# Attention stage: scores in four quarters of the PE array, merge weights sent a step earlier, a shorter end

## Chip, cores and metric

The kernel runs on one core of a Trainium2 chip. The metric is the time of one execution in microseconds of device time; a run's figure is the median of its executions. Lower is better.

## What is computed

A two-layer trunk on 1024 tokens of width 1024. Layer 0 is a gated short convolution, layer 1 dilated sliding-window attention in three groups (window and dilation 128/1, 512/4, 2048/16), 16 heads of 64 in each. The change lies in layer 1.

```python
def dilated_group_attention(q, k, v, bias_tab, window, dilation):
    # the sequence is split into `dilation` residue classes, each cut into 128-query blocks
    logits = einsum('brhnqd,brhnkd->brhnqk', qs, kb) * HEAD_DIM ** -0.5   # kb: past block and own block
    step = BLOCK + a - kk                                                 # a: query row, kk: 0..255
    valid = (step >= 0) & (step <= span) & (key_pos >= 0)                 # span = window // dilation = 128
    logits = where(valid, logits + bias, -inf)
    lse = logsumexp(logits, axis=-1)
    out = einsum('brhnqk,brhnkd->brhnqd', exp(logits - lse[..., None]), vb)
    return out, lse

def dilated_attention_mixer(h, w_in, q_gain, k_gain, w_out, rel_bias):
    ...
    alpha = softmax(stack(lses, axis=0), axis=0)          # merge weights of the three groups
    o = sum(alpha[..., None] * stack(outs, axis=0), axis=0)
    return (o * silu(z)) @ w_out
```

A query row `a` of a block sees keys `a` to `a + 128` of the 256 in past and own block.

## The kernel before

All data lie with features on the partitions. The convolution layer and the projections of the attention layer run first (three-product fp32r matmuls of fast matrix schemes); they write queries, keys (`qkd`), values (`vd`) and gates (`zd`) to DRAM. Then the attention stage follows, whose order is written by hand: the code emits instructions in the order in which each engine shall run them.

Work is cut into 24 units: head pair `hp` (0 to 7, two heads in partitions 0 to 63 and 64 to 127) by group `g` (0 to 2). Units of groups 0 and 1 have four steps of two blocks, group 2 has two steps of four blocks: ten steps a head pair, 80 in all, numbered k. In group 0 all blocks but the first have a past block, in group 1 four of eight, in group 2 none (`alone`). Each step has three parts at fixed distances (lags):

- A (lag 0): scores, one matmul for each block and head: 64 rows of the head (the two heads in the two row halves of PE), 128 queries as weights, 128 or 256 keys as moving columns, into banks `ps` (pool `sp`, three banks, two used by a step). DVE adds the bias and takes the row maxima (L899, `xs`, `nl`), ACT exponentiates and sums (L902). The bias is -1e30 on keys outside the window.
- B (lag `LB` = 2): PE transposes (L909, `pt`, two banks), ACT and DVE copy to `pts` (L847, L849).
- C (lag `LC` = 4): values times `pts` into `po` (L928, and L922 for group 2, 128 rows by 64 columns, the heads in the two column halves); the last step of a half copies `po` to `O` (L939, `finish`).

The rest of a head pair is hung on the last step of its group 2 (`end`) with lags: `store` (maxima and sums to DRAM `nld`, and for group 2 back as `ml` in another layout, L945 on POOL's queue), `weights` (L959 to L963, DVE and ACT), `shares` (L972 to L977), `store_shares` (`fo` to DRAM `fd`), `spread(w)` (two broadcast DMAs of 256 KB from `fd` to `fb`, L985, pool `fbp` of two buffers), `scale(w)` (O times `fb`, DVE, L988), `add(w)` (POOL, L991), `gate` (times SiLU of z, DVE, L994), `high` and `low` (split for the three products, ACT L998 and DVE L1001). The last head pair spreads with PE instead (`wide`, `spread_last`, `last`).

The output projection is done in four parts of two head pairs (`some`, `dense`: six matmuls L1069 to L1071 a tile of 128 x 512, 16 tiles), one tile a step from `LD` steps after the first step of the next even head pair on; DVE adds each tile to `acc` (L1105, `add_sums` at the start of the next step). So steps 0 to 33, 50 to 53 and 70 to 73 have no dense products. Within a step the lags run in the order 0, 1, 4, 3, 5 to 14, 2, then the dense tile, then loads. After the last step the loop goes on until all lags and tiles are out, two tiles a step, with free score, transpose and output banks as further accumulators; then the last two head pairs (kt 6 and 7) are multiplied and closed, tile by tile.

Of the kernel before, what the change touches and what calls it, by code (L numbers as in the profile page):

```python
# [10 lines left out]
F32 = mybir.dt.float32  # L11
# [24 lines left out]
def trunk(ctx: ExitStack, tc: tile.TileContext, a, out):  # L36
# [775 lines left out]
    wp = ctx.enter_context(tc.tile_pool(name="wp", bufs=4, reuse_waits="tile"))  # L812
    with tc.tile_pool(name="sp", bufs=3, space=PSUM) as sp, tc.tile_pool(name="ptp", bufs=2, space=PSUM) as ptp, \
            tc.tile_pool(name="opp", bufs=2, space=PSUM) as opp, tc.tile_pool(name="pp1", bufs=1, space=PSUM) as pp1, \
# [21 lines left out]
        def load_v(hp, g):  # L836
            VS[hp, g] = ap.tile([P, 8, P], F32, name="V", tag="V", bufs=3)
            for q in range(2):
                nc.sync.dma_start(VS[hp, g][:, 4 * q:4 * q + 4].rearrange("p a b -> p (a b)"), vd[hp, g, q])

        O = {}
# [9 lines left out]
        def attention(hp, g):  # L851
# [21 lines left out]
            def make(js, first):  # L873
# [3 lines left out]
                def A():  # L877
                    if first:
                        begin()
                    q, k = QK[hp, g]  # L880
                    ps = [sp.tile([P, 4, P], F32, name="ps", tag="ps") for _ in range(2)]
                    todo = []
                    for n, j in enumerate(js):
                        alone = g == 2 or (j == 0 if g == 0 else j < 4)
                        x0, nk = (n if g == 2 else 2 * n), 1 if alone else 2
                        b = 2 * (j % 4) + j // 4 if g == 1 else j
                        vb = [b] if alone else [b - 1, b]
                        kv = slice(vb[0] * P, (b + 1) * P)
                        for s, hs in enumerate((lo, up)):
                            out_ = ps[s][:, x0:x0 + nk].rearrange("p a b -> p (a b)")  # L890
                            nc.tensor.matmul(out_, q[hs, b * P:(b + 1) * P], k[hs, kv], start=True, stop=True)  # L891
                        todo.append((x0, nk, j, slice(0 if nk == 2 or g == 2 else 128, 256 if nk == 2 or g < 2 else 128)))
                        c.extend((x0 + i, j, vb[i], i == 0, i == nk - 1) for i in range(nk))
# [88 lines left out]
            def spread(w):  # L982
                fb = u["fb", w] = fbp.tile([P, S], F32, name="fb", tag="fb")
                for s, hs in enumerate((lo, up)):
                    nc.gpsimd.dma_start(fb[hs], fd[hp, w, s][None, :].to_broadcast([64, S]))  # L985
# [28 lines left out]
            def spread_last(hf):  # L1014

                hs = slice(64 * hf, 64 * hf + 64)
                for w in (2, 1, 0):
                    fb = u["fb", w] = sp.tile([P, 4, P], F32, name="ps", tag="ps").rearrange("p a b -> p (a b)")
                    for r in range(8):
# [68 lines left out]
        def bank(name):  # L1088
            if name in ("pd", "po"):
                return (pp1 if name == "pd" else opp).tile([P, HALF], F32, name=name, tag=name)  # L1090
            pool = sp if name == "ps" else ptp
            return pool.tile([P, 4, P], F32, name=name, tag=name).rearrange("p a b -> p (a b)")

# [28 lines left out]
        for i, (dt, hf) in enumerate(tiles):  # L1122
            when(4 + i, residual, dt, hf)
        for r in range(3):
            k0 = at[2 * r + 2, 0][0] + LD
            k = k0
            for i, (dt, hf) in enumerate(tiles):
                late = k >= len(steps)
                name = "pd" if not late else ("pd", ("ps", "ps", "pt", "pt")[min(k - len(steps), 3)])[i % 2]
                extra.setdefault(k, []).append(lambda r=r, dt=dt, hf=hf, name=name:  # L1130
                                               some((2 * r, 2 * r + 1), dt, hf, name))
                k += i % 2 if late else 1
        for kt in range(KT):
            k = at[kt // 2 * 2 + 2, 0][0] + LD - 4 + kt % 2 if kt < 6 else len(steps) - 5 + kt % 2
            when(k - 4 - kt % 2, fetch, kt)
            when(k, split, kt)
            when(k + 1, split_low, kt)
        for f in begins.pop(-1):
            f()
        k = 0  # L1140
        while k < len(steps) + LC or any(x >= k for x in extra):
            add_sums()
# [102 lines left out]
```

## Time and profile before

| | us |
|---|---|
| median of 3 runs | 1992.55 |
| lowest and highest run | 1991.82, 1994.5 |
| the profiled execution | 1993.42 |
| its span | 1991.5 |
| PE busy | 1942.4 (98%) |
| DVE busy | 1484.1 (75%) |
| ACT busy | 903.5 (45%) |
| POOL busy | 885.3 (44%) |

The profile is of one execution. Busy shares are means over very different stages; the attention stage starts at 1625.89 us. A matmul of f32 stands as two records, a transpose as one. An engine's idle time is put down to what ended last before its next instruction; a record's own duration is longer than the distance to the next, since matmuls are pipelined, so costs on PE are read from start to start.

### The profile page before, as it was taken

What the parts mean: (1) busy time and instruction counts of PE and PEld (TensorE: products, weight loads), DVE (VectorE), ACT (ScalarE), POOL (GpSimd) and SP (SyncE); (2) the same over time, 40 slices, a digit from 0 to 9 for tenths busy, and PEclk for the clock granted to TensorE, in tenths of its full rate; (3) what the DMA queues carried; (4) which work ended last, traced back from release to release, by engine and by line L of the source; (5) the groups of instructions that cost most, each with busy time, mean ns of one, the idle gap of its engine ahead of it and who ended that gap; (6) DMA issues with size and microseconds to landing.
All of it is one profiled execution on the core that took longest, in us unless ns stands there. A gap on an engine that the chain in (4) does not pass through costs nothing.

```text
span 1991.5 us, 29494 instructions
## 1 busy us (share of the span) xinstructions
PE 1942.4 (98%) x10302; PEld 1579.2 (79%) x10302; DVE 1484.1 (75%) x2751; ACT 903.5 (45%) x2042; POOL 885.3 (44%) x800
## 2 busy tenths in 40 slices
PE   8999999999999999999999999999999998899998
PEld 6888888888887888788887888788888876677776
DVE  6866665666666555898888788878899856787886
ACT  6433333333335344534343434343443448777770
POOL 0356767667665112444455444544454442222330
PEclk9999999999999999999999999999999999999999
DMA  6313232232225565323333323332433278767752
GB/s 198 113 62 96 71 106 85 85 106 70 89 77 176 165 235 171 118 85 106 106 106 117 96 96 117 107 105 85 127 99 106 93 239 259 206 174 219 207 142 85
DMA packets 116805, 254.25 MB, mean 128 GB/s; under 512 B 15822, under 2 KB 22718, under 8 KB 116656
## 3 DMA queue, kind: packets, MB, share of 16 engines
q1 hardware_dynamic: 93024, 177.42, 28.4%
q0 software_dynamic: 23632, 74.95, 12.5%
q8 instruction: 81, 1.33, 0.3%
q14 instruction: 68, 0.56, 0.1%
HBM read 193.05 MB, written 67.64 MB: 131 GB/s over the span
## 4 chain that ended last, share of the span: by engine, by line
PE 77%; DVE 10%; issue 5%; DMA 4%; ACT 2%; POOL 1%; SPq 0%; DVEq 0%; POOLq 0%; ACTq 0%
PE pp L301 18%; PE pp L304 18%; PE pp L303 18%; PE pp L552 3%; PE pp L553 3%; PE pp L551 3%; DVE ws L165 2%; PE pt L909 2%; PE ps L891 2%; DMA nld<-nl 1%; DVE blkc L711 1%; PE pp L374 1%; PE pp L376 1%; PE pp L375 1%; PE po L928 1%
## 5 line engine op out<-in xcount | busy, mean ns | idle before, releaser
L165 DVE TENSOR_TENSOR ws<-wr,ws 128x512 fp32r<-128x512 f32 x284 | 265.3, 936 | 115.5 <-ACT ws L164 114.6
L164 ACT ACTIVATE ws<-wr 128x512 fp32r<-128x512 f32 x284 | 178.3, 629 | 360.4 <-PE pp L304 236.7
L276 POOL TENSOR_TENSOR sr<-wr 128x512 f32<-128x512 f32 x136 | 192.6, 1416 | 264.6 <-DMA wr<-in_conv_w_in 69.7
L164 ACT ACTIVATE ws<-sr 128x512 fp32r<-128x512 f32 x272 | 169.7, 629 | 285.5 <-PE pp L304 236.2
L165 DVE TENSOR_TENSOR ws<-sr,ws 128x512 fp32r<-128x512 f32 x272 | 227.6, 845 | 80.4 <-ACT ws L164 77.6
L313 DVE TENSOR_TENSOR f<-pp,f 128x512 f32<-128x512 f32 x204 | 139.5, 684 | 90.2 <-PE pp L304 83.3
L902 ACT ACTIVATE xs<-xs,nl 128x128 f32<-128x128 f32 (+1 forms) x384 | 167.9, 439 | 68.9 <-DVE nl L899 57.7
L309 ACT ACTIVATE f<-pp 128x512 f32<-128x512 f32 x228 | 132.7, 582 | 28.4 <-POOL blkc L683 14.5
L899 DVE CUSTOM_DVE_ANT_0 xs<-ps,bt 128x128 f32<-128x128 f32 (+1 forms) x384 | 110.9, 347 | 27.5 <-PE ps L891 16.3
L716 POOL DMA_DIRECT2D qkd<-blkc x96 | 68.1, 717 | 131.6 <-DVE blkc L711 123.0
L674 ACT ACTIVATE f<-f 128x512 f32<-128x512 f32 x96 | 60.7, 633 | 140.2 <-DVE f L313 103.1
L276 POOL TENSOR_TENSOR sr<-wr,sr 128x512 f32<-128x512 f32 x68 | 88.9, 1307 | 65.7 <-issue 43.4
L301 PE MATMUL pp<-blkg,ws 128*128 128x512 f32 x272 | 107.3, 394 | 4.3 <-ACT f L309 4.2
L301 PE MATMUL pp<-blkf,ws 128*128 128x512 f32 x272 | 108.5, 399 | 0.7 <-ACT f L309 0.7
L301 PE MATMUL pp<-blka,ws 128*128 128x512 f32 x272 | 107.1, 394 | 0.7 <-ACT f L309 0.7
L301 PE MATMUL pp<-blkb,ws 128*128 128x512 f32 x272 | 107.4, 395 | 0.0
L301 PE MATMUL pp<-blkd,ws 128*128 128x512 f32 x272 | 107.0, 393 | 0.0
L304 PE MATMUL pp<-blkf,ws 128*128 128x512 f32 x272 | 106.3, 391 | 0.0
L304 PE MATMUL pp<-blkd,ws 128*128 128x512 f32 x272 | 106.0, 390 | 0.0
L304 PE MATMUL pp<-blka,ws 128*128 128x512 f32 x272 | 106.0, 390 | 0.0
L304 PE MATMUL pp<-blkb,ws 128*128 128x512 f32 x272 | 106.0, 390 | 0.0
L301 PE MATMUL pp<-blke,ws 128*128 128x512 f32 x272 | 106.0, 390 | 0.0
(329 smaller groups left out, 5388.0 us busy)
## 6 DMA issues: line engine op xcount, KB each, us to landing
wr<-in_conv_w_in SPq DMA_DIRECT2D x128, 256.0 KB, 3.0
wr<-in_wqk SPq DMA_DIRECT2D x96, 256.0 KB, 3.1
qkd<-blkc POOLq DMA_DIRECT2D x96, 256.0 KB, 3.1
qk<-qkd SPq DMA_DIRECT2D x48, 512.0 KB, 8.6
wr<-in_conv_w_out SPq DMA_DIRECT2D x64, 256.0 KB, 3.1
f<-in_x SPq DMA_DIRECT2D x48, 256.0 KB, 4.3
wr<-in_wv SPq DMA_DIRECT2D x48, 256.0 KB, 3.0
vd<-f POOLq DMA_DIRECT2D x48, 256.0 KB, 2.5
```

What stands on the lines that cost most here:

```text
L164: nc.scalar.activation(t[:, 0], src, AF.Copy)
L165: nc.vector.tensor_tensor(t[:, 1], src, t[:, 0].bitcast(F32), op=OP.subtract)
L276: nc.gpsimd.tensor_tensor(t, x, y, op=op)
L301: nc.tensor.matmul(ps, w[:, 0, ws], b[:, k, 0], start=new and k == 0, stop=False, skip_group_check=not new)
L303: nc.tensor.matmul(ps, w[:, 0, ws], b[:, k, 1], start=False, stop=False, skip_group_check=not new)
L304: nc.tensor.matmul(ps, w[:, 1, ws], b[:, k, 0], start=False, stop=end and k == 3, skip_group_check=not new)
L309: nc.scalar.activation(t, ps, AF.Copy)
L313: nc.vector.tensor_tensor(m, ps, m, op=OP.add)
L674: nc.scalar.activation(sq, t, AF.Square)
L716: nc.gpsimd.dma_start(qkd[hp, g, which].rearrange("p (c s) -> p c s", c=c) [:, :, hf * m:(hf + 1) * m], o.rearrange("p (c s) -> p c s", c=c))
L899: nc.vector.tensor_tensor_reduce(out=x, in0=ps[s][:, x0:x0 + nk].rearrange("p a b -> p (a b)"), in1=u["bt"][s][:, bs], op0=OP.add, op1=OP. ...
L902: nc.scalar.activation(x, x, AF.Exp, bias=nm, scale=-1.0, accum_out=L)
```

## The change

1. Scores of a block with a past block: instead of one 128 x 256 matmul a head, two of 64 queries by the 192 keys that these can see; head s uses row half s, query half h column half h. The 64 x 64 places of a bank that are no longer written keep older values, and the bias masks them. The three banks become fixed tiles that are used in turn and are zeroed once by DVE.
2. Lags of the merge: `store` of group 2 from 1 to 0, `weights` 3 to 2, `shares` and `store_shares` 4 to 3, the broadcasts of w = 2 and 1 from 4 to 3, of w = 0 from 8 to 3 (into `sqacc`, free by then, instead of a buffer of `fbp`), `scale(0)` and `add(0)` 11 to 10, `high` 13 to 12, `low` 14 to 13.
3. `LD` 14 to 13: dense products and their weights a step earlier. Residual loads at steps 6, 8, ... 36 instead of 4 to 19.
4. The end: value products of the last two steps at lag 3, transposes of the last step in the loop's first step after the 80, weights, shares and spreading of the last head pair one to two steps earlier, other accumulators for the late tiles, one turn of the loop less.

```diff
-    with tc.tile_pool(name="sp", bufs=3, space=PSUM) as sp, ...
+    with tc.tile_pool(name="sp", bufs=1, space=PSUM) as sp, ...
...
+        banks = [sp.tile([P, 4, P], F32, name="ps", tag=f"ps{i}") for i in range(3)]
+        for t in banks:
+            nc.vector.memset(t, 0.0)
...
-                            nc.tensor.matmul(out_, q[hs, b * P:(b + 1) * P], k[hs, kv], start=True, stop=True)
+                            if alone:
+                                nc.tensor.matmul(out_, q[hs, b * P:(b + 1) * P], k[hs, kv], start=True, stop=True)
+                        if not alone:
+
+                            for h in range(2):
+                                for s, hs in enumerate((lo, up)):
+                                    nc.tensor.matmul(ps[s][64 * h:64 * h + 64, x0:x0 + 2].rearrange("p a b -> p (a b)")
+                                                     [:, 64 * h:64 * h + 192],
+                                                     q[hs, b * P + 64 * h:b * P + 64 * h + 64],
+                                                     k[hs, kv.start + 64 * h:kv.start + 64 * h + 192],
+                                                     start=True, stop=True)
...
-                fb = u["fb", w] = fbp.tile([P, S], F32, name="fb", tag="fb")
+                fb = u["fb", w] = fbp.tile([P, S], F32, name="fb", tag="fb") if w else sqacc
...
-            end.setdefault(1, []).append(store)
+            end.setdefault(0 if g == 2 else 1, []).append(store)
             if g == 2:
                 if hp == HP - 1:
-                    todo = [(LB, weights), (3, shares), (3, wide), (LC, lambda: spread_last(0)),
-                            (LC, lambda: last(0, 0)), (LC, lambda: last(0, 1))]
-                    ending.update(spread=spread_last, last=last)
+                    steps[-2][3] = steps[-2].pop(LC)
+                    end[3] = end.pop(LC)
+                    todo = [(2, shares), (2, wide), (3, lambda: spread_last(0)), (3, lambda: last(0, 0)),
+                            (3, lambda: last(0, 1))]
+                    ending.update(turn=end.pop(LB)[0], weights=weights, spread=spread_last, last=last)
                 else:
-                    todo = [(3, weights), (LC, shares), (LC, store_shares), (LC, lambda: spread(2)),
-                            (LC, lambda: spread(1)), (8, lambda: scale(2)), (8, lambda: spread(0)),
-                            (9, lambda: scale(1)), (9, lambda: add(2)), (11, lambda: scale(0)),
-                            (11, lambda: add(0)), (12, gate), (13, high), (14, low)]
+                    todo = [(LB, weights), (3, shares), (3, store_shares), (3, lambda: spread(2)),
+                            (3, lambda: spread(1)), (3, lambda: spread(0)), (8, lambda: scale(2)),
+                            (9, lambda: scale(1)), (9, lambda: add(2)), (10, lambda: scale(0)),
+                            (10, lambda: add(0)), (12, gate), (12, high), (13, low)]
...
-        LD = 14
+        LD = 13
...
-            when(4 + i, residual, dt, hf)
+            when(6 + 2 * i, residual, dt, hf)
```

PE at the border of two head pairs (last step of one, first two of the next), before. `ps<-qk` are scores (rows of output by columns), `po<-pts,V` values, `pt<-ident,xs` transposes.

```order
L891 MATMUL ps<-qk 128x128 x8
L928 MATMUL po<-pts,V 64x128 x4
L909 MATMUL pt<-ident,xs 128x128 x8
L891 MATMUL ps<-qk 128x128 x2
L891 MATMUL ps<-qk 128x256 x2
L928 MATMUL po<-pts,V 64x128 x8
L909 MATMUL pt<-ident,xs 128x128 x8
L891 MATMUL ps<-qk 128x256 x4
```

The same place on PE after the change.

```order
L902 MATMUL ps<-qk 128x128 x8
L948 MATMUL po<-pts,V 64x128 x4
L929 MATMUL pt<-ident,xs 128x128 x8
L902 MATMUL ps<-qk 128x128 x2
L907 MATMUL ps<-qk 64x192 x4
L948 MATMUL po<-pts,V 64x128 x8
L929 MATMUL pt<-ident,xs 128x128 x8
L907 MATMUL ps<-qk 64x192 x8
```

Nothing moved here; each score with a past block became two.

POOL's queue from the stores of head pair 0 to the sums of its groups, before. `nld<-nl` are the stores of maxima, `ml<-nld` their reload, `fd<-fo` the store of the merge weights, `fb<-fd` the broadcasts, `o<-o` the adds.

```order
L950 DMA nld<-nl 512x1x4 x2
L945 DMA ml<-nld 128x64
L980 DMA fd<-fo 128x6x8
L985 DMA fb<-fd 64x1024 x4
L947 DMA nld<-nl 128x8x4
L985 DMA fb<-fd 64x1024 x2
L950 DMA nld<-nl 512x1x4 x2
L991 TENSOR_TENSOR o<-o 128x1024
```

POOL's queue there after the change.

```order
L970 DMA nld<-nl 512x1x4 x2
L965 DMA ml<-nld 128x64
L1000 DMA fd<-fo 128x6x8
L1005 DMA fb<-fd 64x1024 x4
L1005 DMA sqacc<-fd 64x1024 x2
L967 DMA nld<-nl 128x8x4
L970 DMA nld<-nl 512x1x4 x2
L1011 TENSOR_TENSOR o<-o 128x1024
```

The third broadcast moved ahead of both stores of the next head pair.

DVE at the end, from the weights widened for the last spreading to the sums of the late tiles, before. `qk<-fo` widens, `o<-po` copies, `o<-o,ps` scales, `acc<-pd,acc` is a tile's sum.

```order
L1012 COPY qk<-fo 128x1024 x2
L1105 TENSOR_TENSOR acc<-pd,acc 128x512
L1105 TENSOR_TENSOR acc<-pt,acc 128x512
L939 COPY o<-po 128x512 x2
L1027 TENSOR_TENSOR o<-o,ps 128x512 x3
L1030 TENSOR_TENSOR o<-o 128x512 x2
L1031 TENSOR_TENSOR sz<-o,sz 128x512
L1001 TENSOR_TENSOR y_17669<-sz,y_17669 128x1024
```

DVE there after the change.

```order
L1032 COPY qk<-fo 128x1024 x2
L1127 TENSOR_TENSOR acc<-pd,acc 128x512
L1127 TENSOR_TENSOR acc<-ps,acc 128x512
L959 COPY o<-po 128x512 x2
L1047 TENSOR_TENSOR o<-o,ps 128x512 x3
L1050 TENSOR_TENSOR o<-o 128x512 x2
L1051 TENSOR_TENSOR sz<-o,sz 128x512
L1021 TENSOR_TENSOR y_17653<-sz,y_17653 128x1024
```

The order is the same but for the bank that is summed, and it stands one turn of the loop earlier; on PE there are four dense tiles instead of seven between the last scores and the spreading, and six instead of four between that and the products of kt 6.

## Rows read from the trace of the kernel before

**Rows 1.** The page's part 1: busy time and share of the span by engine.
```profile
PE 1942.4 (98%) x10302; PEld 1579.2 (79%) x10302; DVE 1484.1 (75%) x2751; ACT 903.5 (45%) x2042; POOL 885.3 (44%) x800
```

**Rows 2.** By stretch: length, busy PE, PEld, DVE, ACT, POOL, PE clock, DMA share, GB/s.
```profile
1654.87:1744.15 89.28, 77.33 (x835) 59.51 (x834) 63.47 (x284) 72.22 (x276) 24.05 (x27) 0.92 0.81 234
1744.15:1807.06 62.91, 62.48 (x578) 47.95 (x577) 50.83 (x203) 43.95 (x173) 18.21 (x23) 1.00 0.75 212
1807.06:1827.10 20.04, 17.30 (x198) 13.16 (x197) 16.27 (x63) 16.64 (x58) 5.32 (x3) 1.00 0.61 149
```

**Rows 3.** PE in order of time: start, length, line, names, shape, records.
```profile
1659.97 1.09 PE L928 MATMUL po<-pts,V 128*64 128x128 f32 x16
1661.00 1.09 PE L909 MATMUL pt<-ident,xs 128*128 128x128 f32 x8
1662.02 1.13 PE L891 MATMUL ps<-qk 64*128 64x256 f32 x8
1663.09 1.20 PE L922 MATMUL po<-pts,V 128*64 128x64 f32 x32
1664.21 0.87 PE L909 MATMUL pt<-ident,xs 128*128 128x128 f32 x6
```

**Rows 4.** PE in order of time, a step with dense products.
```profile
1752.74 1.14 PE L891 MATMUL ps<-qk 64*128 64x256 f32 x8
...
1755.24 0.47 PE L1069 MATMUL pd<-y,y 128*128 128x512 f32 x1
...
1756.80 0.49 PE L891 MATMUL ps<-qk 64*128 64x256 f32 x2
```

**Rows 5.** Stalls in the early stretch; brackets: idle before, what ended it.
```profile
1683.87 1.23 DVE L988 TENSOR_TENSOR o<-o,fb 128x1024 f32<-128x1024 f32 x1 [4.08 <-DMA fb<-fd]
...
1685.99 2.07 PE L891 MATMUL ps<-qk 64*128 64x128 f32 x14 [3.90 <-DVE nl L899]
...
1697.90 1.09 PE L909 MATMUL pt<-ident,xs 128*128 128x128 f32 x8 [1.53 <-DVE pts L847]
...
1722.85 1.16 PE L891 MATMUL ps<-qk 64*128 64x128 f32 x14 [2.10 <-DVE nl L899]
...
1725.91 1.97 PE L909 MATMUL pt<-ident,xs 128*128 128x128 f32 x8 [1.33 <-ACT pts L849]
```

**Rows 6.** By stretch, as rows 2: three at half clock.
```profile
1684.47:1691.29 6.82, 5.17 (x32) 4.22 (x32) 6.25 (x36) 5.53 (x27) 4.95 (x5) 0.50 1.05 294
1725.42:1732.25 6.83, 6.33 (x37) 4.90 (x38) 5.02 (x28) 5.75 (x25) 2.36 (x1) 0.50 1.07 271
...
1957.52:1960.93 3.41, 3.07 (x7) 2.48 (x8) 0.99 (x3) 0.00 (x0) 0.00 (x0) 0.50 0.00 0
```

**Rows 7.** DVE's waits in the attention stage: us in total, times, longest.
```profile
DVE o L988 <- DMA fb<-fd: 16.4, 10, 4.1
```

**Rows 8.** POOL in order of time around the second store of maxima.
```profile
1686.42 1.56 POOL L950 DMA_DIRECT2D nld<-nl  x2
...
1697.63 0.57 POOL L945 DMA_DIRECT2D ml<-nld  x1 [6.60 <-DMA nld<-nl]
```

**Rows 9.** DMAs issued from 1640 to 1750: count, KB each, median us to landing.
```profile
nld<-nl POOLq DMA_DIRECT2D x6, 8.0 KB, 9.6
ml<-nld POOLq DMA_DIRECT2D x3, 32.0 KB, 5.5
```

**Rows 10.** DVE in order of time in the two windows without dense products.
```profile
1815.60 1.23 DVE L988 TENSOR_TENSOR o<-o,fb 128x1024 f32<-128x1024 f32 x1 [2.20 <-DMA fb<-fd]
...
1902.18 1.23 DVE L994 TENSOR_TENSOR sz<-o,sz 128x1024 f32<-128x1024 f32 x1 [1.87 <-POOL o L991]
```

**Rows 11.** PE and DVE at the end.
```profile
1950.87 1.71 PE L1020 MATMUL ps<-ident,qk 64*128 64x64 f32 x24
1950.94 1.29 DVE L939 COPY o<-po 128x512 f32<-128x512 f32 x2 [0.40 <-PE po L922]
...
1957.86 0.79 PE L1069 MATMUL pd<-y,y 128*128 128x512 f32 x1 [2.34 <-DVE acc L1105]
```

More of the change, by code (lines that the diff above doesn't have):

```diff
@@ L812, in trunk @@
     wp = ctx.enter_context(tc.tile_pool(name="wp", bufs=4, reuse_waits="tile"))
-    with tc.tile_pool(name="sp", bufs=3, space=PSUM) as sp, tc.tile_pool(name="ptp", bufs=2, space=PSUM) as ptp, \
+    with tc.tile_pool(name="sp", bufs=1, space=PSUM) as sp, tc.tile_pool(name="ptp", bufs=2, space=PSUM) as ptp, \
             tc.tile_pool(name="opp", bufs=2, space=PSUM) as opp, tc.tile_pool(name="pp1", bufs=1, space=PSUM) as pp1, \
@@ L839, in load_v, with scores @@
                 nc.sync.dma_start(VS[hp, g][:, 4 * q:4 * q + 4].rearrange("p a b -> p (a b)"), vd[hp, g, q])
+        banks = [sp.tile([P, 4, P], F32, name="ps", tag=f"ps{i}") for i in range(3)]
+        for t in banks:
+            nc.vector.memset(t, 0.0)
+        turns = [0]
+        def scores():
+            turns[0] += 1
+            return banks[turns[0] % 3]
         O = {}
@@ L880, in A @@
                     q, k = QK[hp, g]
-                    ps = [sp.tile([P, 4, P], F32, name="ps", tag="ps") for _ in range(2)]
+                    ps = [scores() for _ in range(2)]
                     todo = []
@@ L1017, in spread_last @@
                 for w in (2, 1, 0):
-                    fb = u["fb", w] = sp.tile([P, 4, P], F32, name="ps", tag="ps").rearrange("p a b -> p (a b)")
+                    fb = u["fb", w] = scores().rearrange("p a b -> p (a b)")
                     for r in range(8):
@@ L1090, in bank @@
                 return (pp1 if name == "pd" else opp).tile([P, HALF], F32, name=name, tag=name)
-            pool = sp if name == "ps" else ptp
-            return pool.tile([P, 4, P], F32, name=name, tag=name).rearrange("p a b -> p (a b)")
+            t = scores() if name == "ps" else ptp.tile([P, 4, P], F32, name=name, tag=name)
+            return t.rearrange("p a b -> p (a b)")
         sums = []
@@ L1128, in trunk @@
                 late = k >= len(steps)
-                name = "pd" if not late else ("pd", ("ps", "ps", "pt", "pt")[min(k - len(steps), 3)])[i % 2]
+                name = "pd" if not late else (("pd", "ps"), ("pd", "ps"), ("pd", "pt"), ("pt", "pd"))[
+                    min(k - len(steps), 3)][i % 2]
+                if i >= 14:
+                    name = "po"
                 extra.setdefault(k, []).append(lambda r=r, dt=dt, hf=hf, name=name:
                                                some((2 * r, 2 * r + 1), dt, hf, name))
-                k += i % 2 if late else 1
+                k += (i % 2 if i < 13 else 0) if late else 1
         for kt in range(KT):
@@ L1137, in trunk @@
             when(k + 1, split_low, kt)
+        when(len(steps), ending["turn"])
+        when(len(steps), ending["weights"])
         for f in begins.pop(-1):
@@ L1140, in trunk @@
         k = 0
-        while k < len(steps) + LC or any(x >= k for x in extra):
+        while k < len(steps) + LC - 1 or any(x >= k for x in extra):
             add_sums()
```

## Prediction

> **What bounds the kernel now.** I read the page's engine shares first [rows 1]: PE is busy for 98% of the span, so the question is which stretches are not held by PE. The change touches only the attention stage (from 1625.89 us on) and three memsets before it, so the busy times were asked for by stretch, cut at the starts of score groups [rows 2]. Three kinds of stretch appear, and the end. From 1654.87 to 1744.15 (24 steps, no dense products of the output projection between them) PE is busy 77.33 of 89.28 us at a mean clock of 0.92, ACT 72.22, DVE 63.47: nobody is full, so there are stalls. From 1744.15 to 1807.06 (dense products in each step) PE is busy 62.48 of 62.91: PE is the bound; the stretch 1827.10 to 1889.97 repeats it. From 1807.06 to 1827.10 the dense products have run out for four steps, DVE does the merging of a head pair there, and PE is idle for 2.7 us; the stretch from 1889.97 repeats that. After the last scores PE waits again, the longest time at 1957.86 [rows 11].
>
> Inside a step [rows 3], PE runs eight transposes (1661.00 to 1662.02, 1.02 us), eight score records (1662.02 to 1663.09, 1.07 us, 134 ns each), sixteen or thirty-two value records (1.03 and 1.12 us). With dense products the step is 4.06 us [rows 4], 1.56 of it six dense matmuls.
>
> The stalls have an owner. At 1683.87 DVE starts a scaling by the merge weights after 4.08 us of waiting for their broadcast, PE gets its next bank of scores only at 1685.99 after 3.90 us, and PE's granted clock is 0.50 (1.2 of 2.4 GHz) from 1684.47 to 1691.29 [rows 5, 6]. In all DVE waits 16.4 us for that broadcast, ten times [rows 7].
>
> **The change part by part.**
> *Scores.* Each block with a past block (88 of them: 7 in group 0 and 4 in group 1 of 8 head pairs) was two matmuls, four records, 0.535 us; it becomes four matmuls, eight records, of 64 queries by 192 keys. No row shows four quarters at once. Rows do show halves. A transpose, a record of 128 streamed columns with the whole array to itself, takes 128 ns; a value record of 128 columns, on 128 rows and one of two column halves, takes 64, and with 64 columns 35 [rows 3]. So two column halves that share all rows run side by side. The scores of today are the other kind, two row halves. If both kinds hold together, twice as many records run at once over three quarters of the columns: 134 x 0.75 / 2 = 50 ns a record, 0.40 us for the eight, 0.135 us less a block. The ends are 35 ns (the quickest record in these rows; 0.255 us less) and 100 ns (quarters that share rows take turns, 134 x 0.75; 0.265 us more). I take 50, worked out from the form that is nearest. A block's 192 keys are the valid ones of its 64 queries. DVE and ACT still pass over 256 columns; nothing is saved there.
> The Trainium skill, page "TensorE: Matmul & The Clock Gate", section "The mechanism" of Part 3, says that a weight load overlaps running matmuls only where its row group differs. By that, two quarters over the same rows would queue. The value records [rows 3] speak against it, since their pairs share all rows and still run at 64 ns; the sum stands on them.
>
> *Dense steps.* Of the 88 blocks 34 lie in steps that PE bounds (15, 15 and 4 in the three dense stretches): 34 x 0.135 = 4.6 us.
>
> *Shares sent sooner.* The merge weights are computed and sent one step earlier, and the third broadcast (w = 0) no longer waits for the first scaling to free a buffer: it has sqacc and is issued behind the other two, five steps earlier. Residual loads, 256 KB each, are spread over 6 to 36 rather than 4 to 19, which lowers the load on the queue there. So the two broadcasts that DVE waited for land about a step (3 us) sooner, the third some 12 us. What goes from the early stretch: 3.90 us of idle PE plus half of the 5.17 busy us at clock 0.50 (2.6); the same around 1725.42, half of 6.33 (3.2) and 2.10 + 1.33 of idle; 1.53 at 1697.90 [rows 5, 6]. Together about 15 us. ACT sets the floor, 72.22 us [rows 2], so no more than 17 can go, and the scores' 29 x 0.135 here are hidden behind ACT; PE would need 77.33 - 5.8 - 3.9 = 68.
> What comes instead: the chain from the maxima of group 1 (nld, stored by POOL) to ml and to the weights on DVE has a step less. In the early stretch nld lands 9.6 us after its issue and ml 5.5 [rows 9]; POOL stood 6.60 us at ml for it, issued only 11.2 us after the store [rows 8], with that store queued behind 512 KB of broadcast, which now goes ahead of it by steps. The store is ready about 1 us into its step; ml is back 1 + 9.6 + 0.6 + 5.5 = 16.7 us into it, or 12.6 if the store lands in the 5.5 us of ml. DVE reaches the weights three steps of 3.1 us plus 3.4 us later, at 12.7. So a wait of 0 to 4 us for each of head pairs 1 and 2, where I take 2.5; behind it on DVE stand the next step's maxima, for which ACT and then PE wait: about 5 us. In dense steps (4.06 us) the same chain has 15.6 us, and little or no wait. On POOL the add for w = 0 is queued behind ml's wait for nld, and DVE's gate behind that add, so they hang on the same landing. Early stretch: 15 - 5 = 10 us gained (bounds 3 and 17).
>
> *The windows without dense products.* DVE waited 2.20 us for a broadcast at 1815.60 and 1.87 us for POOL's add at 1902.18 [rows 10]; with the third broadcast and its scaling earlier, both should be gone: 4 us. The dense products start one step sooner (LD 13), so the window moves by a step; DVE's work in it is the same, 1.22 us a pass, only packed closer (gate, split and weights in one step), so I count nothing for that, from -3 to +3.
>
> *The end.* Before, PE waited 2.34 us at 1957.86 for the pd bank, since its sum stood on DVE behind the scaling, adding and low part of the last head pairs, and then ran 3.07 busy us at clock 0.50 [rows 6, 11], 1.5 us lost. Now the last transposes and value products come two steps sooner among the dense tiles: from the last scores to the spreading on PE stand four tiles instead of seven, from there to the products of kt 6 six instead of four. The order on DVE is the same, 6.9 us from the copies (1950.94) to pd's sum done (1957.86) [rows 11]; PE fills it with the spreading (1.7) and three tiles (3 x 1.5) before it needs pd again, where two stood before. So some 0.7 us of wait is left, and I count no fall of the clock for it. Gain 2.34 + 1.5 - 0.7 = 3 us (0 to 5). One dense tile has left the end for step 73, 1.5 us there against 1.5 here. The last weights come earlier too, some 14 us after their store is ready; if ml were later than that, the sums queued behind on DVE and so the spreading would be late, and these 3 us go.
>
> *Nothing.* Three memsets of the score banks stand on DVE ahead of the projection's last sum, for which DVE waits on PE's products in any case; two 128x512 copies take 1.29 us [rows 11], so the three take 2 us or less, and that is their cost once if the cover is gone.
>
> Sum: 10 + 4.6 + 4 + 3 = 21.6 us. Against the profiled execution, 1993.42, that is 1971.8; the median of the runs shown is 0.9 lower, so **1971 us**.
>
> **The rivals.**
> *Row-sharing quarters take turns* (100 ns a record): dense steps lose 34 x 0.265 = 9 us; in the early stretch PE needs 71.5 + 7.7 = 79 us instead of 68 and takes ACT's place as the floor, leaving 4 of the 10; windows 3, end 3. Net 1 us: 1992. For it: no row shows a quarter. Against: the value records. This is what the rule of the Trainium skill named above would make of the scores.
> *The quarters do not overlap at all* (slower): 201 ns a record, 1.07 us more a block. Dense 36 us, early 102 us of PE against 89 (13), first ten steps 8, windows 10, less 3 at the end: 64 us, 2056. It turns from gain to loss at about 103 ns a record. Against: both kinds of halves run side by side today.
> *The store of the maxima takes the broadcast's place*: where nld and ml stay at 9.6 and 5.5 us, DVE stands 4 us at the weights twice, POOL's add is late for the gate, and PE's clock falls again as at 1684.47. Then 3 of the early 10 are left: 1978. For it: the landing times [rows 9]; against: the broadcast is no longer queued ahead of the store.
> *More is gained*: ACT's floor is reached early (17) and records cost 40 ns: 1960.
>
> **How the numbers follow.** Forecast 0.62 (its own range 1964 to 1976), store of the maxima 0.16 (1978), row-sharing turns 0.12 (1992, as likely above as below), no overlap 0.04 (2056), more gained 0.06 (1960). Below 1960 and above 1990 I leave 0.04 and 0.13, so the range is 1960 to 1990. Faster by over 0.2% (4 us, about what a measurement of this kernel tells from no change): the forecast, the store, more, less a little: 0.83. Within: 0.08. Slower: 0.09.
>
> **What would show it.** Score records: groups of sixteen in 0.8 us (quarters overlap), 1.6 (turns), 3.2 (none). DVE's waits for the broadcast: near 0 instead of 16.4; its waits for ml or for POOL's add in the early stretch: about 5 us; no stretch at clock 0.50 between 1680 and 1735. Dense steps of 3.8 us instead of 4.06. At the end a wait of 1.2 us rather than 2.34 and no half clock. The prediction is wrong if the early stretch, now 89.28 us, does not fall to about 79, or if scores cost more than they did.

## The result

The changed kernel takes 1977.78 us (median of 4 runs, 1973.57 to 1981.87), the kernel before beside it 1992.44 (1991.82 to 1994.5): a ratio of 0.9924, 95% interval 0.9902 to 0.9947. That is 14.7 us faster; 21.4 were forecast. A second measurement gave 1978.31 and 0.9921 (0.99 to 0.9941). The profiled execution of the kernel after is its quickest, 1973.57, so a second profile (1977.58, of the second measurement) stands beside it in this table. Stretches are cut at the starts of the same score groups as [rows 2]; "end" runs to the end of the last matmul. The last four columns are experiments, below.

| us | before | after | after, second | split_early | early_all | lags_only | old_end |
|---|---|---|---|---|---|---|---|
| start of the stage | 1625.89 | 1624.30 | 1627.36 | 1628.94 | 1626.15 | 1628.19 | 1626.96 |
| first ten steps | 28.98 | 27.33 | 28.36 | 28.38 | 28.45 | 27.93 | 27.34 |
| early, 24 steps | 89.28 | 83.25 | 83.08 | 84.27 | 78.52 | 82.47 | 85.13 |
| dense, 15 steps | 62.91 | 60.56 | 60.55 | 60.55 | 60.57 | 63.40 | 61.91 |
| window, 5 steps | 20.04 | 19.34 | 19.33 | 17.68 | 17.68 | 18.02 | 17.84 |
| dense, 15 steps | 62.87 | 60.56 | 60.57 | 60.57 | 60.55 | 64.28 | 62.55 |
| window, 5 steps | 20.04 | 20.20 | 20.19 | 17.67 | 17.68 | 18.02 | 17.84 |
| dense, 5 steps | 20.61 | 19.68 | 19.69 | 19.69 | 19.68 | 23.02 | 22.74 |
| end | 57.13 | 52.77 | 52.89 | 52.82 | 54.42 | 53.69 | 53.77 |

In the kernel after, the early stretch holds one dense tile more than before (1.56 us of PE, step 33), the end one less; lags_only and old_end, with `LD` 14, have it at the end as before. The start of the stage differs between executions of code that is, but for the three memsets, the same up to there (1624.3 to 1628.9), so the 1.6 us by which "after" starts ahead is scatter.

The rows of the page's part 1, and the stretches as in [rows 2] and [rows 6], of the kernel after:

```profile
PE 1925.4 (98%) x10654; PEld 1566.2 (79%) x10654; DVE 1493.2 (76%) x2754; ACT 903.5 (46%) x2042; POOL 880.9 (45%) x800
```

```profile
1651.63:1734.88 83.25, 71.64 (x957) 54.76 (x956) 66.51 (x294) 73.25 (x280) 24.67 (x28) 0.96 0.91 257
1734.88:1795.44 60.56, 60.56 (x638) 46.77 (x637) 48.51 (x192) 43.00 (x168) 17.10 (x22) 1.00 0.86 235
1795.44:1814.78 19.34, 16.45 (x226) 12.28 (x225) 18.98 (x72) 17.42 (x62) 6.72 (x6) 1.00 0.45 150
1875.34:1895.54 20.20, 17.70 (x226) 13.40 (x225) 19.58 (x72) 18.22 (x64) 6.15 (x4) 0.92 0.59 194
1715.64:1722.47 6.83, 5.02 (x35) 3.95 (x36) 2.76 (x10) 4.31 (x16) 2.94 (x2) 0.50 1.04 289
```

PE now fills the dense stretch to the last hundredth (60.56 of 60.56). In the first window DVE nearly does: 18.98 of 19.34 us, where it was 16.27 of 20.04 [rows 2]. The second window has 3.4 us at half clock both before (from 1906.35) and after (from 1889.72), the first has none. In the early stretch the DMA share rose from 0.81 to 0.91, and one stretch at half clock is left where two were.

PE in order of time, a step without dense products ([rows 3] answers to it) and the score groups of a step with them ([rows 4]):

```profile
1657.51 1.09 PE L929 MATMUL pt<-ident,xs 128*128 128x128 f32 x8
1658.53 0.88 PE L907 MATMUL ps<-qk 64*64 64x192 f32 x16
1659.34 1.20 PE L942 MATMUL po<-pts,V 128*64 128x64 f32 x32
...
1742.84 0.88 PE L907 MATMUL ps<-qk 64*64 64x192 f32 x16
...
1746.66 0.56 PE L907 MATMUL ps<-qk 64*64 64x192 f32 x8
```

Sixteen quarter records take 0.81 us from start to start (1658.53 to 1659.34), 50.6 ns each; the dense step is 3.82 us (1742.84 to 1746.66) instead of 4.06.

Waits in the attention stage of the kernel after, DVE's ([rows 7] answers to the third) and then the first rows of PE's: us in total, times, longest.

```profile
DVE xs L919 <- PE ps L907: 14.3, 24, 2.1
...
DVE mx L979 <- DMA ml<-nld: 2.7, 2, 1.9
...
DVE o L1008 <- DMA sqacc<-fd: 0.6, 1, 0.6
```

```profile
PE pt L929 <- ACT pts L859: 11.4, 12, 1.7
PE ps L902 <- DMA qk<-qkd: 3.2, 1, 3.2
```

DVE's wait for the broadcasts is gone (16.4 to 0.6), and it waits 2.7 us for `ml`. What is new is PE's wait for a load of queries and keys, once, 3.2 us (2.3 in the second profile, which has the half clock there too). It comes 20 us after the second head pair's broadcasts, and the clock falls around it. PE in order of time, then the loads issued from 1698 to 1704 (count, KB each, median us to landing; [rows 9]):

```profile
1717.45 0.80 PE L902 MATMUL ps<-qk 64*128 64x128 f32 x4 [3.23 <-DMA qk<-qkd]
```

```profile
fb<-fd POOLq DMA_DIRECT2D x4, 256.0 KB, 9.7
qk<-qkd SPq DMA_DIRECT2D x2, 512.0 KB, 16.5
wraw<-in_wo SPq DMA_DIRECT2D x2, 512.0 KB, 19.8
sqacc<-fd POOLq DMA_DIRECT2D x2, 256.0 KB, 14.6
```

Queries and keys leave at 1698.6 with six broadcasts and two rows of the output weights (`wraw`), 3.5 MB within 5 us, and the later of the two lands after 18.3 us.

### The profile page after: what moved, and what is told of

It reads as the page before. It is cut to its first block, busy times and chain, and to the rows that moved or that the text cites. A ratio compares the mean times of both kernels' runs of the same rounds, so it can differ in the third digit from the quotient of the medians.

```text
span 1971.8 us, 30228 instructions
## 1 busy us (share of the span) xinstructions
PE 1925.4 (98%) x10654; PEld 1566.2 (79%) x10654; DVE 1493.2 (76%) x2754; ACT 903.5 (46%) x2042; POOL 880.9 (45%) x800
## 4 chain that ended last, share of the span: by engine, by line
PE 78%; DVE 12%; issue 4%; DMA 4%; ACT 3%; SPq 0%; POOL 0%; DVEq 0%; POOLq 0%; ACTq 0%
PE pp L301 18%; PE pp L304 18%; PE pp L303 18%; PE pp L552 3%; PE pp L553 3%; PE pp L551 3%; DVE ws L165 2%; PE pt L929 2%; DVE blkc L711 1%; PE pp L374 1%; PE po L948 1%; PE pp L375 1%; PE pp L376 1%; ACT xs L922 1%; DMA wraw<-in_wo 1%
## 5 line engine op out<-in xcount | busy, mean ns | idle before, releaser
L165 DVE TENSOR_TENSOR ws<-wr,ws 128x512 fp32r<-128x512 f32 x284 | 281.2, 992 | 115.5 <-ACT ws L164 113.9
L276 POOL TENSOR_TENSOR sr<-wr 128x512 f32<-128x512 f32 x136 | 185.0, 1360 | 261.1 <-DMA wr<-in_wqk 74.8
L301 PE MATMUL pp<-blkg,ws 128*128 128x512 f32 x272 | 107.0, 393 | 3.4 <-ACT f L309 3.4
L303 PE MATMUL pp<-blkg,ws 128*128 128x512 f32 x272 | 105.9, 389 | 0.0
```

The lines of the kernel that those rows point to most:

```text
L165: nc.vector.tensor_tensor(t[:, 1], src, t[:, 0].bitcast(F32), op=OP.subtract)
L276: nc.gpsimd.tensor_tensor(t, x, y, op=op)
L301: nc.tensor.matmul(ps, w[:, 0, ws], b[:, k, 0], start=new and k == 0, stop=False, skip_group_check=not new)
L303: nc.tensor.matmul(ps, w[:, 0, ws], b[:, k, 1], start=False, stop=False, skip_group_check=not new)
```

## Experiments: which part brings what

**scores_only.** The kernel before with the quarters and the three fixed banks, all lags, loads and the end as before.

> The kernel before with the quarter scores and the three fixed banks alone. Theory: only steps bound by PE gain, 34 blocks x 0.135 = 4.6 us, and the rest is hidden behind ACT and the waits for broadcasts: 1986 to 1988. Rival (every block counts): 88 x 0.135 = 12 us, 1980.

Measured: 1990.51 (1987.31 to 1992.67), ratio 0.9976 (0.9965 to 0.9986), about 4.5 us.

**lags_only.** The kernel before with the new lags, the third broadcast into `sqacc` and the spaced residual loads; `LD` 14, whole scores, the old end.

> The kernel before with the merge's lags, the third broadcast into sqacc and the residual loads of the changed kernel alone; scores, dense start and end as before. Theory: the waits of DVE for broadcasts go (16.4 us before, under 1 in the changed kernel), 6 to 8 us are gained in the early stretch and none in the windows: 1984 to 1987, with runs that spread. Rival (the bunched broadcasts delay the loads by as much as they help): 1990 to 1994.

Measured: 1984.65 (1983.98 to 1987.5), ratio 0.9953 (0.9937 to 0.9968), about 10 us. The early stretch gains 6.8 us, as expected. Each window gains 2.0, where nothing was expected, but the step behind it takes 5.87 us after 4.46 and 3.87 before: window and that step together go from 24.50 and 23.91 to 23.89 each.

**whole_scores.** The kernel after with one matmul a head and block again.

```diff
-                            for h in range(2):
-                                for s, hs in enumerate((lo, up)):
-                                    nc.tensor.matmul(ps[s][64 * h:64 * h + 64, ...], ..., k[hs, ...192], ...)
+                            nc.tensor.matmul(out_, q[hs, b * P:(b + 1) * P], k[hs, kv], start=True, stop=True)
```

> The changed kernel with the scores as one 128 x 256 matmul a head again. Theory: 4.6 to 6 us slower than the changed kernel, 1983. Rival (scores pay in the early stretch too once the waits are gone): 10 to 12 us slower, 1989.

**after_again.** The kernel after, as the measure beside these three.

> The changed kernel once more, as the control of this batch, with a second profile. Theory (the early stretch hangs on loads): the median stays near 1978 and runs spread over some 8 us; the profile shows a wait of PE for queries and keys (3.2 us in the first profile) of another size, with or without a stretch at half clock after it. Rival (the spread comes from the merge chain of maxima): the wait for queries and keys is the same in both profiles and DVE's wait for ml (2.7 us in the first) differs.

Measured: whole_scores 1983.84 (1982.33 to 1985.44), after_again 1978.31 (1977.58 to 1981.89): 5.5 us. From either side the total is about 5, but the stretches do not add up in the same way. whole_scores loses 1.73, 1.71 and 0.50 us in the three dense stretches, 3.9 in all where 4.6 were forecast; the rest lies mainly in the early stretch (85.46 against 83.08) and the end (54.38 against 52.89, with 3.4 us at half clock). In scores_only the three gain only 1.2, 0.2 and 0.3 us: DVE's wait for the broadcasts is 21.9 us there after 16.4, and PE waits 0.7 and 1.3 us for DVE's copies in two of them. That its total is the one forecast is luck. The stretches of whole_scores, dense and window as in [rows 2]:

```profile
1742.01:1804.30 62.29, 62.29 (x578) 48.01 (x577) 48.61 (x192) 43.02 (x168) 16.55 (x21) 1.00 0.87 234
1804.30:1823.63 19.33, 16.94 (x198) 12.82 (x197) 18.97 (x72) 17.42 (x62) 6.65 (x6) 1.00 0.40 130
```

In the dense stretch the quarters bring 62.29 - 60.56 = 1.73 us for 15 blocks, 0.115 a block. In the window they bring nothing: 19.33 with whole scores, 19.34 with quarters. PE isn't what the window waits for.

**keys256.** Four quarters, but all 256 keys in each.

```diff
-                                    ... [:, 64 * h:64 * h + 192], ..., k[hs, kv.start + 64 * h:kv.start + 64 * h + 192],
+                                    ..., k[hs, kv],
```

> The quarters stay, but each takes all 256 keys of its block pair instead of 192, so that only the skipped keys are undone; all else as in the kernel after (1978). Theory A (the array was full before: two row halves of 128 columns use all of it, and four quarters use no more, so that the whole gain on the scores is the 64 keys not computed): a group of sixteen records takes 256/192 of 0.81 us = 1.07 to 1.08 us, as the whole blocks did, and the time goes back to that of the kernel with whole-block scores: 1983 to 1984. Rival B (the quarters themselves run faster, by more overlap of their loads or fills): the group takes under 1.0 us and the time stays at 1978 to 1981.

**rows_adjacent.** The loops over `h` and `s` exchanged, so that the two quarters of the same 64 rows follow each other.

> The four quarters of a block in another order: the two that share the same 64 rows of the array one behind the other, then the other two, where the kernel after alternates the rows; all else as in the kernel after (1978). Theory A (quarters run side by side whatever they share, as the profile of the kernel after has 50.6 ns a record with each pair of rows shared at a distance of one): sixteen records in 0.81 us again, 1978. Rival B (a load of weights or a multiplication waits for the one before it on the same rows, as the Trainium skill has it, page TensorE: Matmul & The Clock Gate, Part 3, The mechanism): pairs take turns, up to 100 ns a record and 1.6 us for sixteen; 36 to 58 of these groups by 0.8 us give 2000 to 2020.

Measured: keys256 1983.04 (1979.95 to 1983.56); rows_adjacent 1979.54 (1978.62 to 1982.66). PE in order of time, a group of sixteen and what follows it, first of keys256, then of rows_adjacent:

```profile
1747.60 1.09 PE L907 MATMUL ps<-qk 64*64 64x256 f32 x16
1748.63 1.09 PE L947 MATMUL po<-pts,V 128*64 128x128 f32 x16
```

```profile
1748.81 0.88 PE L907 MATMUL ps<-qk 64*64 64x192 f32 x16
1749.62 1.09 PE L948 MATMUL po<-pts,V 128*64 128x128 f32 x16
```

With 256 keys the sixteen take 1.03 us (1747.60 to 1748.63), 64 ns a record, and the kernel is back at the time with whole scores. The eight records of whole blocks took 1.07 [rows 3]: two row halves of 128 columns had the whole array in use already, quartering it adds next to nothing (0.04), and the gain is the 64 keys not computed. It takes quarters to leave them out, since each half of the queries skips other keys. With the rows shared by neighbours the sixteen take 0.81 us as before: quarters don't queue for their rows. The rule of the Trainium skill that the prediction weighed (page "TensorE: Matmul & The Clock Gate", Part 3, "The mechanism") is not borne out here; it speaks of weight loads, and that a multiplication waits for its rows as well is the expectation's reading of it.

## Experiments: the windows

The table has the first window at 19.34 after 20.04, with the waits of [rows 10] gone. Two explanations: ScalarE's order (`high` now stands on ACT in the gate's own step, with the copies behind it), or DVE and ACT are simply full there. The trace of the kernel after already speaks against the first: ACT starts `high` without a wait in both windows (1807.22 and 1887.12), and the 2.1 us that the expectation of high13 puts there stand at 1927.54, past them.

**high13.** `high` one step later.

```diff
-                            (10, lambda: add(0)), (12, gate), (12, high), (13, low)]
+                            (10, lambda: add(0)), (12, gate), (13, high), (13, low)]
```

> The high part of the gated output (a ScalarE copy) is queued one step after the gate instead of behind it in the same step; all else as in the kernel after (1978). Theory A: in the two windows without dense products ScalarE stands up to 2.1 us on VectorE's gate with the copies of transposed weights behind it, and TensorE waits 1.75 us for one of these copies in each; with the high part a step later both windows (19.3 and 20.2 us) get 1.5 to 2 shorter: 1974 to 1975. Rival B: VectorE has become the bound of the windows (busy 18.98 of 19.34 us in the first), so that ScalarE's order doesn't matter: 1978, windows at 19 to 20 us. Rival C: the low part now waits on VectorE for the high part of the same step, and the first dense product a step on waits for it: 1979 to 1981.

Measured: 1986.69 (1981.06 to 1993.96), 8 us slower than the kernel after; the windows 20.76 and 22.32, and the end 57.46, with 6.8 us at half clock. This order costs: `low` now waits on DVE for ACT's `high` of the same step, and a dense tile stands behind it. So the run alone doesn't rule out that another order would help. DVE in order of time:

```profile
1816.00 1.23 DVE L1021 TENSOR_TENSOR y<-sz,y 128x1024 fp32r<-128x1024 f32 x1 [1.02 <-ACT y L1018]
```

**split_pool.** The low parts of six rows of the output weights on POOL instead of DVE.

```diff
-            nc.vector.tensor_tensor(W[kt][:, 1], raws[kt], W[kt][:, 0].bitcast(F32), op=OP.subtract)
+            (nc.gpsimd if kt < 6 else nc.vector).tensor_tensor(W[kt][:, 1], raws[kt], ...)
```

> The low parts of the output weights (a subtraction of 128x1024, 1.2 to 1.65 us each on VectorE, two in each window) go to GpSimd for the first six of the eight rows; all else as in the kernel after (1978). Theory A (VectorE bounds the windows, busy 18.98 of 19.34 us): two subtractions less, 2.4 to 2.9 us, in each of the three places; both windows come down to 17 to 18 us and the last step of the early stretch too: 1971 to 1974. Rival B (ScalarE's order bounds the windows): the gate still comes when it came, windows 19 to 20 us, 1978. Rival C: on GpSimd a subtraction takes 2.4 us as its additions do and stands between them and the gate that waits for the last addition: 1979 to 1982.

Measured: 1981.36 (1979.68 to 1982.79), 3 us slower; windows 20.18 and 19.59, early stretch 85.55. This did not tell the two apart, since DVE's time did not fall: it is busy 19.11 us in the first window. The rows of POOL and of DVE in order of time show one reason:

```profile
1812.47 2.98 POOL L1105 TENSOR_TENSOR y<-wraw,y 128x1024 fp32r<-128x1024 f32 x1 [0.32 <-ACT y L1102]
```

```profile
1813.16 2.33 DVE L979 TENSOR_TENSOR mx<-ml 128x16 f32<-128x16 f32 x1
1815.52 0.17 DVE L980 TENSOR_TENSOR mx<-mx,nl 128x16 f32<-128x16 f32 x1
```

An operation on 16 columns, 0.16 us in the kernel after, takes 2.33 and ends at 1815.49, as POOL's subtraction does (1815.45). The Trainium skill, page "SBUF — State Buffer", section "SBUF: two separate sides", says that VectorE and GpSimd share a port pair that one instruction holds to its end; this row agrees, and so does DVE's gate at 1727.87, 5.67 us instead of 1.21 while two such subtractions run on POOL.

**split_early.** The same work stays on its engines but goes elsewhere: rows 2 to 5 of the output weights are loaded and split five steps earlier, in dense steps.

```diff
-            k = at[kt // 2 * 2 + 2, 0][0] + LD - 4 + kt % 2 if kt < 6 else len(steps) - 5 + kt % 2
+            k = at[kt // 2 * 2 + 2, 0][0] + LD - (4 if kt < 2 else 9) + kt % 2 if kt < 6 else len(steps) - 5 + kt % 2
```

> The output weights' rows 2 to 5 are loaded and split five steps earlier, into dense steps in which TensorE is full and VectorE and ScalarE idle 1.2 to 1.8 us each, out of the two windows; all else as in the kernel after (1978). Theory A (in the windows VectorE, 18.98 of 19.34 us busy, and ScalarE, 17.4, have become the bound): 2.4 to 2.9 us of VectorE and 2.1 of ScalarE less in each window, which come down from 19.3 and 20.2 to 17 to 18, the dense steps stay at 60.6: 1973 to 1975. Rival B (ScalarE's wait for VectorE's gate, and not the amount of work, holds up the copies): windows stay at 19 to 20: 1978. Rival C: the weights come late there or push VectorE's and ScalarE's work in the dense steps behind TensorE's: the dense steps grow by 1 to 2 us each, 1978 to 1980.

Measured: 1975.36 (1972.88 to 1976.21), ratio 0.991 (0.989 to 0.9929). Dense stretch and window:

```profile
1741.59:1802.14 60.55, 60.55 (x637) 46.77 (x636) 50.87 (x195) 44.92 (x170) 17.10 (x22) 1.00 0.87 237
1802.14:1819.82 17.68, 16.02 (x225) 12.30 (x224) 16.32 (x70) 15.64 (x60) 6.71 (x6) 1.00 0.49 158
```

2.4 us of DVE's work and 1.9 of ACT's went into the dense stretch, which takes 60.55 as before; the window lost 2.7 and 1.8 and is 1.66 us shorter, the second one 2.5. Three steps inside the first window, in the kernel after and in split_early:

```profile
1798.14:1809.76 11.62, 9.11 (x132) 6.60 (x131) 11.37 (x38) 11.62 (x40) 2.92 (x2) 1.00 0.37 123
1804.84:1815.40 10.56, 8.90 (x132) 6.62 (x131) 9.40 (x40) 9.87 (x38) 2.92 (x2) 1.00 0.40 130
```

There ACT is busy for all of the 11.62 us and DVE for 11.37. With whole_scores this shows that in the windows the work on DVE and ACT is the bound, not PE and not a wait of ACT for the gate. Which of the two engines it is stays open, since the split moves work of both.

## Experiments: the early stretch and the end

**w0_lag6.** The third broadcast three steps later, all else as after.

```diff
-                            (3, lambda: spread(1)), (3, lambda: spread(0)), (8, lambda: scale(2)),
+                            (3, lambda: spread(1)), (6, lambda: spread(0)), (8, lambda: scale(2)),
```

> The broadcast of the first set of shares (w = 0, into sqacc) goes out three steps later, at 6 instead of 3 steps after the pass; all else as in the kernel after (1978). Theory A: in the stretch without dense products the three broadcasts of a head pair, 512 KB each, leave together and delay the next head pair's queries and keys; TensorE waits 2.3 to 3.2 us for them once and runs 6.8 us at half clock behind it. With the third broadcast later that wait and that half-clock stretch go, and the stretch of 24 steps (83.1 to 83.3 us in two profiled runs of the kernel after) takes 78 to 80: 1973 to 1975 in all. Rival B: the DMA engines are simply full there (0.91 of their time), so that the queries come no earlier whatever the order: the wait stays at 2 to 3 us, 1978. Rival C: the broadcast is then late for the multiplication by the shares two steps on (10 less 6 less its landing), and VectorE waits for it as before the change: 1980.

Measured: 1977.53 (1975.87 to 1978.58), no different from the kernel after. PE's wait for queries fell to 0.90 us, but 1.74 for a copy of transposed scores came right ahead of it, the 6.83 us at half clock stayed, and the early stretch took 82.61. The broadcasts that leave together are not enough to explain that place. Nor is the wait for queries: it is 0.9 us in keys256, 0.4 in split_pool and none in whole_scores and lags_only, and their early stretches take 84.44, 85.55, 85.46 and 82.47 us, the last without the extra tile.

```profile
1719.15 1.09 PE L929 MATMUL pt<-ident,xs 128*128 128x128 f32 x8 [1.74 <-DVE pts L857]
1721.15 0.80 PE L902 MATMUL ps<-qk 64*128 64x128 f32 x4 [0.90 <-DMA qk<-qkd]
```

ACT, too, waits for a load there in the kernel after, 2.52 us for a row of the output weights, which `LD` 13 asks for a step sooner:

```profile
1720.07 1.06 ACT L1102 ACTIVATE y<-wraw 128x1024 fp32r<-128x1024 f32 x1 [2.52 <-DMA wraw<-in_wo]
```

**early_all.** split_early, the third broadcast at 6 as in w0_lag6, and rows 0 and 1 of the output weights five steps earlier as well, so that they leave at 1684.6, ahead of the crowd. The edit to the weights, against split_early:

```diff
-            k = at[kt // 2 * 2 + 2, 0][0] + LD - (4 if kt < 2 else 9) + kt % 2 if kt < 6 else len(steps) - 5 + kt % 2
+            k = at[kt // 2 * 2 + 2, 0][0] + LD - 9 + kt % 2 if kt < 6 else len(steps) - 5 + kt % 2
```

> As split_early (1975.4), and besides rows 0 and 1 of the output weights (512 KB each) are loaded and split five steps earlier too, in the early stretch, and the broadcast of the first set of shares goes out 6 steps after the pass instead of 3. Theory A (in the early stretch the DMA engines are the bound, 0.91 of their time, and the queries of the head pair that TensorE waits 2.3 to 4.5 us for are held up by the two weight rows, 20 us from issue to landing, and the broadcasts that left together): the wait and the 6.8 us at half clock behind it go, together up to 3 + 3.4 us; the early stretch (83.3 to 84.3) takes 78 to 80 and the whole 1970 to 1972. Rival B (what is moved ahead delays other loads as much, V or the head pair before): 1974 to 1977, with another wait for a load in its place. Rival C (not the loads but ScalarE and VectorE, busy 73 and 67 of 83 us, bound that place): the wait for queries goes, but one for copies of transposed weights takes its place: early stretch 81 to 83, 1973 to 1976.

Measured: 1968.88 (1967.92 to 1971.01), ratio 0.9881 (0.9861 to 0.9901): quicker than both kernels. The early stretch:

```profile
1654.60:1733.12 78.52, 69.26 (x957) 52.89 (x956) 66.65 (x294) 72.36 (x280) 24.82 (x28) 1.00 0.93 274
```

The clock is full throughout and PE's wait for queries is down to 0.2 us, while DVE and ACT are as busy as in the kernel after (66.51, 73.25). What differs in this stretch is when these loads leave, and the split of two rows with them; it is 4.6 us shorter than in the second profile of after. Against the first (83.25, PE busy 71.64) about half of the gain is PE's busy time, without the half clock, and half its idle time. Which of the two moves did it is not separated: the early weights without the later broadcast were not run.

**old_end.** The kernel after with `LD` 14, the old places of the last weights and the old end.

> The kernel after with the old end: dense products 14 steps behind their head pairs instead of 13, their sums in the old banks, two more in the last steps, the last weights at the old places. Theory A (by the profiles): the end is 4.3 us shorter in the kernel after, 1.5 of which is one dense product that now stands in the early stretch, so that the old end costs 2.5 to 3.5 us net: 1980.5 to 1982, with the 2.3 us wait for a bank of sums and 3.4 us at half clock back. Rival B: what the end gained is only the moved product, 1978 to 1979.

Measured: 1982.85 (1981.66 to 1986.54), 4.5 us slower. By stretches hardly any of that is the end. From step 34 to the last matmul it takes 236.65 us, the second profile of after 233.22. Of the difference of 3.43, 1.85 lies in the steps 34 to 68, in which only `LD` differs (142.30 against 140.45). From step 69 on it takes 94.35 against 92.77, and 1.56 of that is the tile that stands earlier in the kernel after. In rows_adjacent, which has the new end and no half clock there, these steps take 91.91; so the new end is worth 0 to 0.9 us. Neither expected sign came back: the clock does not fall at the end, and PE's longest wait for the `pd` bank is 1.4 us, as in lags_only, which has the old end too (first old_end, then lags_only):

```profile
PE pd L1089 <- DVE acc L1125: 1.4, 1, 1.4
PE pd L1069 <- DVE acc L1105: 1.4, 1, 1.4
```

The early stretch is longer too, 85.13 us without that tile against 83.08 with it; why is not shown.

## Why the prediction held, and where it missed

The time lies in the range given, 1960 to 1990, but not in the forecast's own, 1964 to 1976, and by the prediction's own sign, an early stretch of about 79 us, it failed there. The rival "the store of the maxima takes the broadcast's place" had 1978, the number measured, and that is luck too. The clock did fall once, as that rival had it, but DVE stands 0.8 and 1.9 us at the weights in the early stretch, not 4 twice.

**Scores, right in size.** Forecast 50 ns a record and 4.6 us in PE-bound steps; measured 50.6 ns and 3.9 us in the three dense stretches (whole_scores), 0.115 a block instead of 0.135. The bound that rows set, the value records of [rows 3], was the right witness against row-sharing turns, which rows_adjacent rules out.

**Waits for the broadcast, right.** 16.4 us became 0.6. The wait for `ml` was put at 2.5 us twice; it is 2.7 in two waits together.

**Early stretch, 10 us forecast, 7.6 to 7.8 measured** (6.0 to 6.2 with the tile's 1.56 counted against it). The step that failed is "what comes instead". It followed the chain of the maxima on the queues, whose waits came out smaller than feared, but not what else would hold PE there: a wait of 3.2 us for the next head pair's queries, 18.3 us from issue to landing among three broadcasts and two weight rows, and 6.8 us at half clock around it. "No stretch at clock 0.50 between 1680 and 1735" was wrong. early_all, which moves the weight rows with their split and the third broadcast, gets 4.6 us of it back; which of these is the cause stays open. The wait for queries alone is not: lags_only, where PE never waits for them, gains no more (6.8).

**Windows, 4 us forecast, 0.5 measured** (0.70 and -0.16); with the dense step behind each, which is 4.46 and 3.87 before and 3.87 after, 1.1. The step that failed is "both should be gone: 4 us": a wait's length was taken as the gain. DVE's waits of 2.20 and 0.72 us in the first window are gone, but the work behind them, on DVE (18.98 of 19.34 us) and ACT (17.42), could not get through sooner. lags_only shows it without the move of `LD`: its windows lose the 4 us, the steps behind them take back all but 0.6. In the kernel after, the same cut holds 2.7 us more of DVE's work than before, since the steps in it hold two more copies of outputs, the shares and a low part. With its bounds for packing, -3 to +3, the prediction had 1 to 7: 0.5 lies outside, 1.1 just inside.

**Dense stretches.** 2.35 and 2.31 us, of which the quarters are 1.73; 0.6 is the first step of each, as above.

**End, 3 us forecast, 2.7 to 2.8 measured** (4.2 to 4.4 less the moved tile). The size is right largely by luck. The prediction gave the gain to the new order at the end, but with the old one lags_only is already 3.1 us ahead of the kernel before from step 69 on, and old_end leaves 0 to 0.9 for the new one. PE waits 0.98 us for the `pd` bank, where 0.7 was worked out ([rows 11]: 2.34); of the 1.4 us less, 0.9 came with the lags:

```profile
1938.59 0.50 PE L1091 MATMUL pd<-y,y 128*128 128x512 f32 x1 [0.98 <-DVE acc L1127]
```

In sum: forecast 10 + 4.6 + 4 + 3 = 21.6; the second profile has 1991.5 - 1975.8 = 15.7 in spans, and the medians 14.7. The two misses, 2.3 us early and 3.5 in the windows, are the two that early_all and split_early take up.

## What to carry to other kernels

The length of a wait is the gain from removing it only if the engines around it have room: read each engine's busy time in that stretch, and where the next one is within a few per cent of the length, move its work into a stretch that another engine bounds. A transfer that is sent sooner lands among others; list what is issued within the same few us, and who waits for the last of it. Splitting a matmul over array parts pays only by the columns it lets one skip if the parts in use already filled the array.

## What the runs showed of the chip that was not expected

- Among 3.5 MB issued within 5 us, a 512 KB load of queries and keys landed after 18.3 us; the median of these loads from 1640 to 1750 was 6.3.
- A subtraction on GpSimd held a VectorE operation of 0.16 us for 2.33, to its own end (split_pool). Work moved from VectorE to GpSimd left VectorE as busy as before in the first window there (19.11 us after 18.98).
- At the end the clock fell in some kernels and not in others, after the same waits of 0.98 and 1.15 us: end 52.8 us in after and split_early, 54.4 in w0_lag6 and early_all, whose granted clock was 0.50 for 3.4 us there. It did not fall in lags_only and old_end either, with a wait of 1.4. What decides it stays open.
